# Regrouping the opening of a one-core decoder layer: groups of 2, 3, 5 and 6 row blocks instead of 2, 4, 6 and 4

## The chip, the cores and the metric

The kernel runs on 1 core of one Trainium2 chip. The metric is the device time of one execution in microseconds (us). A core has TensorE (PE; its weight loads are listed apart as PEld), VectorE (DVE), ScalarE (ACT), GpSimd (POOL) and SyncE (SP), which here only issues DMAs, and 16 DMA engines that all issuing queues share.

## The reference, cut to what matters

The layer is SwiGLU, token mixing, SwiGLU, each behind an RMS norm that is modulated by a conditioning vector c. The change lies in the first of the three:

```python
SEQ, D_MODEL, D_FF, N_MOD = 256, 2048, 5632, 9
c_act = jax.nn.silu(c)
mod = (c_act @ w_ada[l] + b_ada[l]).reshape(b, N_MOD, D_MODEL)
h = modulate(rms_norm(x, norm_ffn1[l]), mod[:, 0], mod[:, 1])
x = x + 0.5 * mod[:, 2][:, None, :] * swiglu(h, w_ffn1_gu[l], w_ffn1_down[l])
h = modulate(rms_norm(x, norm_mix[l]), mod[:, 3], mod[:, 4])
...
def swiglu(h, w_gu, w_down):
    gate, up = jnp.split(h @ w_gu, 2, axis=-1)
    return (jax.nn.silu(gate) * up) @ w_down
```

h has 256 rows and 2048 columns, that is 16 blocks of 128 columns ("row blocks" of the weight). All is float32. A matmul is made of three products of split operands: a weight tile is cast to a shorter float on ACT (the high half, `wh`), the rest is subtracted on DVE (`wl`), and TensorE adds `wh*hh`, `wh*hl` and `wl*hh`.

## The kernel before, in words

**Conditioning.** One output m (of nine) of `c_act @ w_ada` is 16 rows of w_ada's transposed layout, each 128 partitions by 2048 numbers, 1 MB. `ada_load` (L211) loads such a row, `ada_pass` (L217, its instruction is L220) multiplies a part of it by `cact` on DVE and sums it; a row takes one, two or four passes. `ada_end` (L234) adds the bias. Outputs 0 and 1 are needed block by block before h's blocks exist; outputs 2, 4 and 3 are needed later and are worked off by a pacemaker: `tick()` (L318) adds `pace["rate"]` and, for every whole one, takes a step of `conditioning` (L266), which is one pass of a quarter row and, ahead of it, the load of the row that it will want.

**The opening (L976 to L1306)** makes the first 8 of 11 column chunk pairs of h @ w_gu before all of h exists. It goes over h in groups of blocks, `bounds = (0, 2, 6, 12, 16)` (L1164). In each group the loop at L1260 visits 16 chunks of 512 columns (8 gate, 8 up; two of them are made apart in the first group). A visit loads that chunk's weights for the group's blocks (`load_blocks`, L1170, up to four blocks in a buffer), splits them in pieces of two blocks (`split`, L371: the cast is L375, the subtraction L377), and multiplies (`products`, L354, matmul L360): 6 matmuls a block. Between groups a chunk's sums are kept in SBUF: `to_parts` (L1231, copies at L1234) moves the two banks of a chunk out, and `open_banks` (L1196, copies at L1206) copies them back into PSUM before the next group adds to them. Both copies run on ACT.

**While a group is multiplied, the next group's h is made**, by the generator `group` (L1080): for each block two rows of w_ada (outputs 1 and 0), each with two passes of 1024 numbers (one of 2048 in the first group), then two blocks at a time `ada_end`, the modulation (L628) and the split of h (`parts_of_h`, L633; L636 and L637). Blocks below `TURNED = 6` are turned on TensorE (`turned_x`, L1041), later ones come turned from HBM and are scaled on POOL (`normed_columns`, L1070). The rows lie in `ring`, two places of one row each (L980). While the group before the last is multiplied (`alone`, L1249), the rows of outputs 0 and 1 use one of the two places only, since the pacemaker's rows use the other (`place`, L996, and `place_early`, L1243). In the last group the pacemaker's rows lie in weight buffers, of which there are four (`RAWS`).

**The last group** ends each pair of chunks with `swiglu_up` (L706): the kept sums are added on DVE (L720, L721), then Silu on ACT (L724), the product on DVE (L725), and the result is turned. Turned by DMA it takes three steps that `later` (L651) spreads over the following visits: ACT takes the 16-bit halves apart (L535), SP issues a DMA transpose (`back<-flat`, L540), ACT puts them together (L551). There are three `flat` and four `back` tiles. `turn_step` (L326) takes one step of all such work after every visit, and after every weight load of the later stages. The other way, `transpose_to` (L514), is four TensorE transposes (L518) and a copy out of PSUM (L519).

**Who sets the order.** SP's instructions run in the order in which the program is written (L103). The other engines' instructions are put in order by the framework's scheduler from its own times and the order of the text, and run in that order; `issue_after(i)` puts an instruction behind `i` on the same engine. Behind the opening `ffn_up` (L734) makes chunk pairs 8 to 10 with whole weights (`load`, L349) and then `down_product` (L753) follows. `Ahead` (L695) loads the first of `ffn_up`'s weights within the opening's last visit.

Accumulators are four PSUM banks (`psa`), two for each chunk.

Of the kernel before, what the change touches and what calls it, by code (L numbers as in the profile page):

```python
# [9 lines left out]
F32 = mybir.dt.float32  # L10
# [3 lines left out]
ALU = mybir.AluOpType  # L14
# [3 lines left out]
P = 128  # L18
S = 256
# [58 lines left out]
def layer_kernel(  # L78
# [615 lines left out]

    class Ahead:  # L695


        def __init__(self, raw):
            self.raw, self.made = raw, {}

        def __getitem__(self, h):
            if h not in self.made:
                self.made[h] = split(wsp, "w", self.raw[:, 2 * h : 2 * h + 2, :], CH)
            return self.made[h]

    def swiglu_up(banks_g, banks_u, tiles, ci, parts=None, by_dma=False, behind=(None, None)):  # L706

        def held_back(which):
            return nullcontext() if behind[which] is None else tc.issue_after(behind[which])

        k0 = ci * KB
        dest = tiles[k0 // KD].rearrange("p (k s) -> p k s", s=S)
        kk = k0 % KD
        work = []
        for t in range(NT):
            s = t512()
            g, u = banks_g[t], banks_u[t]
            if parts is not None:
                with held_back(1):
                    nc.vector.tensor_add(s, g, parts[0][t])  # L720
                    nc.vector.tensor_add(parts[1][t], u, parts[1][t])  # L721
                g, u = s, parts[1][t]
            with held_back(0):
# [12 lines left out]

    def ffn_up(held, w, tiles, first, bg=None, turned=(), ahead=None, head=None):
        for ci in range(first, DFF // CH):
            bg = bg or gemm(held, w, [ci * CH], ahead=head)[0]
            bu = gemm(held, w, [DFF + ci * CH], ahead=ahead)[0]  # L740
            swiglu_up(bg, bu, tiles, ci, by_dma=ci in turned)
            bg = ahead = head = None

# [296 lines left out]

    def turned_x(k0):  # L1041

        xn = [t512()[:, : 2 * P] for _ in range(NT)]
        for t in range(NT):
            nc.scalar.mul(xn[t], x_sb[:, t, k0 * P : (k0 + 2) * P], r[:, t : t + 1])
        turned = [bank()[:, :S] for _ in range(2)]
        for i in range(2):
# [21 lines left out]

    def normed_columns(k0):  # L1070

        xt = t512()
        both = xt.rearrange("p (k s) -> p k s", s=S)
        nc.sync.dma_start(both, x_t[k0 : k0 + 2].rearrange("k p s -> p k s"))
        nc.gpsimd.tensor_tensor(
            out=both, in0=both, in1=root_row[0][:, None, :].broadcast_to([P, 2, S]), op=ALU.mult
        )
        return [xt[:, i * S : (i + 1) * S] for i in range(2)]

    def group(ks, passes=2):  # L1080

        for k0 in ks[::2]:
            srcs = normed_columns(k0) if k0 >= TURNED else None
            for k in (k0, k0 + 1):
                for m in (1, 0):
                    if (m, k) not in rows_of:
                        place(m, k)
                    for q in range(passes):
                        ada_pass(k, rows_of[m, k], early[m], q, passes)
                    yield  # L1090
            for m in (1, 0):
                ada_end(m, slice(k0, k0 + 2), early[m], 0 if m else None, passes)
            h = t512()
            for i, src in enumerate(srcs or turned_x(k0)):
                modulated(h[:, i * S : (i + 1) * S], k0 + i, src, 0)
            parts_of_h(held, k0, h)

    banks, moved, unlinted, fresh = {}, set(), set(), set()
    for n, one_bank in zip(firsts, (acc_bank, side_bank)):
# [19 lines left out]
    with tc.manual_schedule(engines=ORDERED):  # L1119
# [76 lines left out]
    def open_banks(n, sums):  # L1196
        seeded = sums and n in moved
        banks[n] = [acc_bank() for _ in range(NT)]
        unlinted.discard(n)
        fresh.add(n)  # L1200
        if seeded:
            unlinted.add(n)
            fresh.discard(n)
            for b, p in zip(banks[n], part_of(n)):
                with tc.issue_after(cast[-1]):
                    nc.scalar.copy(b, p)  # L1206
# [24 lines left out]
    def to_parts(n):  # L1231
        for p, b in zip(part_of(n), banks.pop(n)):
            with tc.issue_after(cast[-1]):
                nc.scalar.copy(p, b)  # L1234
        moved.add(n)

# [11 lines left out]
    for g, ks in enumerate(groups):  # L1248
        alone.append(g == len(groups) - 2)  # L1249
        del alone[:-1]  # L1250
        final = g == len(groups) - 1
        if g == len(groups) - 2:
            set_pace(ROWS_FFN1, 192, place_early, 0)
        if final:
            pace["rate"], pace["ahead"] = 2 / 3, 1
        order = chunks if (len(groups) - g) % 2 else chunks[::-1]
# [3 lines left out]
        for i, n in enumerate(order):  # L1260
            if g == 0 and n in firsts:
                continue
            visit(n, ks, n not in stay, g == len(groups) - 2 or final and i < 12, final or (g == len(groups) - 2 and n in stay))
            if g:
# [3 lines left out]
                for m, ms in after:  # L1268
                    ready(m, ms)
                    if m not in banks and not final:  # L1270
                        open_banks(m, not (g == len(groups) - 2 and m in stay))
                if not after:
                    head = Ahead(load(gu, 0, EARLY * CH))
                    head[0]
            if final:
# [21 lines left out]
            elif n % 2:  # L1297
# [489 lines left out]
```

## Time and profile before

| | |
|---|---|
| median of 3 runs | 2366.71 us (2365.81 to 2366.98) |
| the profiled execution's own time | 2367.18 us |
| its span, first to last instruction | 2365.0 us |
| mean granted TensorE clock | 0.997 |
| DVE busy | 1672.1 us (71%) |
| ACT busy | 1373.5 us (58%) |
| HBM read | 598.47 MB, 255 GB/s over the span |
| weight loads of two and of four row blocks | 30 of 512 KB, 160 of 1024 KB |

In the tables of stretches ("windows") each row gives the stretch in us from the span's start, its length, the busy time of PE, PEld, DVE, ACT and POOL with the number of instructions, the mean granted TensorE clock, the DMA engines' busy share and the GB/s moved. In the timeline a row is: start, length, engine, line, operation, output<-input, count, and in brackets the idle time of that engine just before and what ended it. Matmuls overlap, so a matmul's length is more than its share of the stream. In lists of groups, after the bar stand the busy time in us and the mean length of one in ns.

### The profile page before, as it was taken

Reading aid. Unit: us, or ns where it says so; the run is one execution under the profiler, and the core shown is the slowest. Engines: PE = TensorE matmul, PEld = TensorE weight load, DVE = VectorE, ACT = ScalarE, POOL = GpSimd, SP = SyncE. Lnnn points to the kernel's source line nnn. Section 1 sums busy time; section 2 is a strip of 40 time slices with the busy share of each in tenths; the row PEclk is TensorE's granted clock in tenths of the full one; section 3 lists DMA queues with packets and bytes.
Section 4 is the critical chain, followed back from the end, with each engine's and each line's share of the span. In section 5 each row is a group of like instructions: output and inputs, shape, how many; then the busy total and the mean of one; then the engine's idle time right before and its main releaser. Section 6 shows DMA issues by size and latency. Waiting matters only on the chain.

```text
span 2365.0 us, 28346 instructions
## 1 busy us (share of the span) xinstructions
PE 2336.4 (99%) x10429; PEld 1917.8 (81%) x10429; DVE 1672.1 (71%) x2576; ACT 1373.5 (58%) x1900; POOL 17.4 (1%) x27
## 2 busy tenths in 40 slices
PE   8999998999999999999999999999999999999998
PEld 5888886888888888778888888888888888888887
DVE  7788886778867768975777776677655555545656
ACT  6766566555546568775556564465455455455544
POOL 0000000000000000000000000000000000000000
PEclk9999999999999999999999999999999999999999
DMA  9988979988776898877678887754767777776553
GB/s 385 375 326 352 363 240 294 373 308 318 271 259 247 265 289 230 259 226 244 267 269 307 295 288 286 289 206 185 242 238 255 251 241 256 224 235 204 193 198 125
DMA packets 196124, 631.27 MB, mean 267 GB/s; under 512 B 117329, under 2 KB 118993, under 8 KB 125457
## 3 DMA queue, kind: packets, MB, share of 16 engines
q1 hardware_dynamic: 193490, 618.46, 75.1%
q0 software_dynamic: 1600, 9.83, 1.3%
q8 instruction: 81, 1.33, 0.2%
q10 hardware_dynamic: 896, 1.19, 0.1%
q14 instruction: 57, 0.47, 0.1%
HBM read 598.47 MB, written 4.22 MB: 255 GB/s over the span
## 4 chain that ended last, share of the span: by engine, by line
PE 96%; DMA 2%; DVE 1%; ACT 1%; issue 0%; SPq 0%; DVEq 0%; ACTq 0%
PE pa L360 94%; DMA raw<-in_w_ffn_gu_dram 1%; PE ps L1471 0%; DVE slot L220 0%; DMA slot<-in_w_ada_dram 0%; PE pd L1387 0%; DMA back<-flat 0%; ACT wh L375 0%; DMA x_sb<-in_x_dram 0%; PE ps L360 0%; DVE wl L377 0%; PE ps L910 0%; PE ps L1387 0%; PE pd L1571 0%; PE pd L1556 0%
## 5 line engine op out<-in xcount | busy, mean ns | idle before, releaser
L377 DVE TENSOR_TENSOR wl<-raw,wh 128x1024 fp32r<-128x1024 f32 x792 | 963.1, 1226 | 518.8 <-ACT wh L375 452.9
L375 ACT CAST wh<-raw 128x1024 fp32r<-128x1024 f32 x792 | 829.6, 1054 | 799.9 <-PE pa L360 739.7
L360 PE MATMUL pa<-wh,hh 128*128 128x512 f32 x2184 | 599.4, 392 | 11.7 <-ACT wh L375 9.2
L360 PE MATMUL pa<-wh,hl 128*128 128x512 f32 x2184 | 594.2, 390 | 0.0
L360 PE MATMUL pa<-wl,hh 128*128 128x512 f32 x2184 | 587.7, 390 | 0.1
L360 PEld LDWEIGHTS pa<-wh,hh 128*128 128x128 f32 x2184 | 407.9, 188 | 101.7 <-ACT wh L375 13.5
L360 PEld LDWEIGHTS pa<-wh,hl 128*128 128x128 f32 x2184 | 410.4, 188 | 86.5 <-issue 0.4
L360 PEld LDWEIGHTS pa<-wl,hh 128*128 128x128 f32 x2184 | 410.0, 188 | 87.0 <-DVE wl L377 0.8
L360 PE MATMUL pa<-wh,a 128*128 128x512 f32 x1824 | 452.3, 389 | 0.0
L360 PEld LDWEIGHTS pa<-wh,a 128*128 128x128 f32 x1824 | 341.5, 188 | 70.6
L360 PE MATMUL pa<-wl,a 128*128 128x512 f32 x912 | 245.1, 389 | 0.0
L220 DVE CUSTOM_DVE_ANT_0 slot<-slot,cact 128x512 f32<-128x512 f32 (+2 forms) x292 | 221.9, 812 | 14.5 <-DMA slot<-in_w_ada_dram 14.3
L360 PEld LDWEIGHTS pa<-wl,a 128*128 128x128 f32 x912 | 171.1, 188 | 35.5
L551 ACT COPY slot<-back 128x512 uint16<-128x512 uint16 x156 | 104.0, 766 | 0.0
L535 ACT COPY flat<-t 128x512 uint16<-128x512 uint16 x144 | 81.3, 617 | 29.7 <-DMA back<-flat 21.2
L220 DVE CUSTOM_DVE_ANT_0 rows_x<-rows_x,cact 128x512 f32<-128x512 f32 x124 | 78.8, 688 | 24.7 <-DMA rows_x<-in_w_ada_dram 24.5
L410 ACT CAST a<-slot 128x512 fp32r<-128x512 f32 x114 | 70.6, 621 | 28.5 <-PE pa L360 28.3
L411 DVE TENSOR_TENSOR a<-slot,a 128x512 fp32r<-128x512 f32 x114 | 78.0, 686 | 0.1
L220 DVE CUSTOM_DVE_ANT_0 raw<-raw,cact 128x512 f32<-128x512 f32 (+1 forms) x88 | 58.2, 711 | 20.1 <-DMA raw<-in_w_ada_dram 20.1
L1234 ACT COPY slot<-pa 128x512 f32<-128x512 f32 x72 | 38.6, 589 | 22.3 <-PE pa L360 22.1
L360 PE MATMUL pa<-wh,home 128*128 128x512 f32 x160 | 39.5, 389 | 0.0
L220 DVE DVE_READ_ACCUMULATOR2_ANT sums<- 128x1 f32 x440 | 36.7, 83 | 0.0
(230 smaller groups left out, 1079.8 us busy)
## 6 DMA issues: line engine op xcount, KB each, us to landing
raw<-in_w_ffn_gu_dram SPq DMA_DIRECT2D x160, 1024.0 KB, 5.8
raw<-in_w_in_dram SPq DMA_DIRECT2D x104, 1024.0 KB, 6.2
slot<-in_w_ada_dram SPq DMA_DIRECT2D x88, 1024.0 KB, 7.3
raw<-in_w_ffn_down_dram SPq DMA_DIRECT2D x88, 1024.0 KB, 4.9
rows_x<-in_w_ada_dram SPq DMA_DIRECT2D x31, 1024.0 KB, 7.1
raw<-in_w_ada_dram SPq DMA_DIRECT2D x21, 1024.0 KB, 5.9
raw<-in_w_swa_branch_dram SPq DMA_DIRECT2D x16, 1024.0 KB, 5.7
raw<-in_w_ret_branch_dram SPq DMA_DIRECT2D x16, 1024.0 KB, 6.0
```

What stands on the lines that cost most here:

```text
L220: nc.vector.tensor_tensor_reduce(out=w[:, at], in0=w[:, at], in1=cact[:, at], scale=1.0, scalar=0.0, op0=ALU.mult, op1=ALU.add, accum_out= ...
L360: product = nc.tensor.matmul(banks[t], act[:, j, t * P : (t + 1) * P], weights[:, j, :], start=starts and i == 0 and j == 0, stop=ends and ...
L375: cast.append(nc.scalar.copy(hi, src).ins)
L377: low.append(nc.vector.tensor_sub(lo, src, hi.bitcast(F32)).ins)
L410: nc.scalar.copy(hi, v)
L411: nc.vector.tensor_sub(lo, v, hi.bitcast(F32))
L535: nc.scalar.copy(planes[:, i, :], words(src)[:, :, i])
L551: nc.scalar.copy(into[:, :, :, i], held["turned"][:, i])
L1234: nc.scalar.copy(p, b)
```

## The change

The groups become 2, 3, 5 and 6 blocks; the helpers learn to take an odd block; `TURNED` becomes 5. In the second group, four of the 16 chunks (2, 6, 10, 14) are not copied back into PSUM but start afresh, and their kept sums are added on DVE when they leave. The pacemaker runs at half a step per piece in the third group (24 passes instead of 48) and at one step per piece in the first 8 visits of the last (24 passes; before, 2/3 of a step in 12 visits of two pieces, 16 passes); the 16 passes over are left to the stages behind. In the last group the additions are no longer held behind the next visit's first subtraction (L718, L1305), pairs 6 and 7 are turned on TensorE, and `Ahead`, the early load for `ffn_up`, goes.

```diff
-        nc.scalar.copy(held.hi[:, k : k + 2, :], h)
-        nc.vector.tensor_sub(held.lo[:, k : k + 2, :], h, held.hi[:, k : k + 2, :].bitcast(F32))
+        ks = slice(k, k + h.shape[1])
+        nc.scalar.copy(held.hi[:, ks, :], h)
+        nc.vector.tensor_sub(held.lo[:, ks, :], h, held.hi[:, ks, :].bitcast(F32))
...
-    class Ahead:
...
             if parts is not None:
-                with held_back(1):
-                    nc.vector.tensor_add(s, g, parts[0][t])
-                    nc.vector.tensor_add(parts[1][t], u, parts[1][t])
+                nc.vector.tensor_add(s, g, parts[0][t])
+                nc.vector.tensor_add(parts[1][t], u, parts[1][t])
...
-    TURNED = 6
+    TURNED = 5
...
         for k0 in ks[::2]:
-            srcs = normed_columns(k0) if k0 >= TURNED else None
-            for k in (k0, k0 + 1):
+            nk = min(2, ks[-1] + 1 - k0)
+            srcs = normed_columns(k0, nk) if k0 >= TURNED else None
+            for k in range(k0, k0 + nk):
...
-    bounds = (0, 2, 6, 12, 16)
+    bounds = (0, 2, 5, 10, 16)
...
         seeded = sums and n in moved
+        if seeded and n in by_vector:
+            added.add(n)
+            seeded = False
...
         for p, b in zip(part_of(n), banks.pop(n)):
+            if n in added:
+                with tc.issue_after(low[-1]):
+                    nc.vector.tensor_add(p, p, b)
+                continue
             with tc.issue_after(cast[-1]):
                 nc.scalar.copy(p, b)
...
+        by_vector = chunks[2::4] if g == 1 else ()
         if g == len(groups) - 2:
-            set_pace(ROWS_FFN1, 192, place_early, 0)
+            set_pace(ROWS_FFN1, 2 * 192, place_early, 0)
         if final:
-            pace["rate"], pace["ahead"] = 2 / 3, 1
+            pace["rate"], pace["ahead"] = 1.0, 1
...
-            visit(n, ks, n not in stay, g == len(groups) - 2 or final and i < 12, final or (g == len(groups) - 2 and n in stay))
+            visit(n, ks, n not in stay, g == len(groups) - 2 or final and i < 8, final or (g == len(groups) - 2 and n in stay))
...
-                if not after:
-                    head = Ahead(load(gu, 0, EARLY * CH))
-                    head[0]
...
                     (part_of(n - 1), part_of(n)),
-                    True,
-                    (cast[-1], low[-1]),
+                    n // 2 < 6,
+                    cast[-1],
...
-    pace["rate"] = (192 - 64) / 117
+    pace["rate"] = (192 - 48) / 117
     pace["ahead"] = AQ
-    ffn_up(held, gu, tiles, EARLY, turned=range(EARLY, DFF // CH), head=head)
+    ffn_up(held, gu, tiles, EARLY, turned=range(EARLY, DFF // CH))
```

More of the change, by code (lines that the diff above doesn't have):

```diff
@@ L693, in later_at_once, with swiglu_up @@
                 yield
-    class Ahead:
[L698 to L709, printed above, removed]
+    def swiglu_up(banks_g, banks_u, tiles, ci, parts=None, by_dma=False, behind=None):
         k0 = ci * KB
@@ L718, in swiglu_up @@
             if parts is not None:
-                with held_back(1):
-                    nc.vector.tensor_add(s, g, parts[0][t])
-                    nc.vector.tensor_add(parts[1][t], u, parts[1][t])
+                nc.vector.tensor_add(s, g, parts[0][t])
+                nc.vector.tensor_add(parts[1][t], u, parts[1][t])
                 g, u = s, parts[1][t]
-            with held_back(0):
+            with nullcontext() if behind is None else tc.issue_after(behind):
                 nc.scalar.activation(s, g, AF.Silu)
@@ L735, in swiglu_up, with ffn_up @@
             turns.append(later(work))
-    def ffn_up(held, w, tiles, first, bg=None, turned=(), ahead=None, head=None):
+    def ffn_up(held, w, tiles, first, bg=None, turned=(), ahead=None):
         for ci in range(first, DFF // CH):
-            bg = bg or gemm(held, w, [ci * CH], ahead=head)[0]
+            bg = bg or gemm(held, w, [ci * CH])[0]
             bu = gemm(held, w, [DFF + ci * CH], ahead=ahead)[0]
             swiglu_up(bg, bu, tiles, ci, by_dma=ci in turned)
-            bg = ahead = head = None
+            bg = ahead = None
     ORDERED = {mybir.EngineType.PE, mybir.EngineType.DVE, mybir.EngineType.Activation}
@@ L1039, in square, with turned_x @@
         )
[L1041 to L1043 removed]
+    def turned_x(k0, nk=2):
+        xn = [t512()[:, : nk * P] for _ in range(NT)]
         for t in range(NT):
[L1045 to L1047 removed]
+            nc.scalar.mul(xn[t], x_sb[:, t, k0 * P : (k0 + nk) * P], r[:, t : t + 1])
+        turned = [bank()[:, :S] for _ in range(nk)]
+        for i in range(nk):
             for t in range(NT):
@@ L1091, in group @@
             for m in (1, 0):
-                ada_end(m, slice(k0, k0 + 2), early[m], 0 if m else None, passes)
-            h = t512()
-            for i, src in enumerate(srcs or turned_x(k0)):
+                ada_end(m, slice(k0, k0 + nk), early[m], 0 if m else None, passes)
+            h = t512()[:, : nk * S]
+            for i, src in enumerate(srcs or turned_x(k0, nk)):
                 modulated(h[:, i * S : (i + 1) * S], k0 + i, src, 0)
             parts_of_h(held, k0, h)
-    banks, moved, unlinted, fresh = {}, set(), set(), set()
+    banks, moved, unlinted, fresh, added = {}, set(), set(), set(), set()
     for n, one_bank in zip(firsts, (acc_bank, side_bank)):
```

11 lines of the change are left out of this document (6 added, 5 removed).

## The prediction

> **What bounds the kernel now.** I read the page first, then the busy time by stretches, then what TensorE waited for, then the timeline around the longest wait.
>
> ```profile
> PE 2336.4 (99%) x10429; PEld 1917.8 (81%) x10429; DVE 1672.1 (71%) x2576; ACT 1373.5 (58%) x1900; POOL 17.4 (1%) x27
> ```
>
> TensorE is the bound; with a span of 2365.0 us it idles 28.6 us in all, and no more can be won without taking matmuls away, which the change does not. In stretches (the opening's four groups are about 20-69, 69-156, 156-287 and 287-377):
>
> ```profile
> 20.00:69.00 49.00, 47.04 (x190) 34.36 (x189) 41.49 (x50) 35.21 (x55) 0.00 (x0) 1.00 0.98 383
> 69.00:156.00 87.00, 87.00 (x386) 72.03 (x385) 71.43 (x99) 64.69 (x97) 4.63 (x3) 1.00 0.93 368
> 156.00:287.00 131.00, 130.81 (x577) 107.81 (x576) 108.83 (x189) 77.56 (x106) 3.28 (x2) 1.00 0.88 348
> 287.00:377.00 90.00, 88.83 (x391) 72.78 (x390) 74.64 (x117) 60.89 (x81) 0.00 (x0) 1.00 0.84 263
> 377.00:408.00 31.00, 22.95 (x88) 18.41 (x89) 18.79 (x33) 19.43 (x29) 2.17 (x4) 0.83 1.01 290
> 408.00:720.00 312.00, 312.00 (x1377) 258.00 (x1377) 242.64 (x408) 172.43 (x209) 0.00 (x0) 1.00 0.83 306
> ```
>
> Between 20 and 408 TensorE idles 1.96 + 0 + 0.19 + 1.17 + 8.05 = 11.4 us; from 408 to 720 nothing. Its waits, and the largest of them in the timeline:
>
> ```profile
> PE pa L360 <- ACT wh L375: 9.2, 5, 7.3
> PE pa L360 <- DVE t L720: 1.9, 2, 1.1
> ```
> ```profile
> 393.31 1.09 PE L360 MATMUL pa<-wl,hh 128*128 128x512 f32 x4
> 401.68 2.07 PE L360 MATMUL pa<-wh,hh 128*128 128x512 f32 x4 [7.27 <-ACT wh L375]
> 403.55 1.91 PE L360 MATMUL pa<-wh,hl 128*128 128x512 f32 x4
> 405.26 1.91 PE L360 MATMUL pa<-wl,hh 128*128 128x512 f32 x4
> 406.97 1.26 PE L360 MATMUL pa<-wh,hh 128*128 128x512 f32 x4
> ```
> ```profile
> 63.49 215.32 PE pa L360 x948
> ```
> ```profile
> 396.00:400.00 4.00, 0.00 (x0) 0.00 (x0) 0.00 (x0) 1.14 (x2) 0.00 (x0) 0.64 1.12 280
> 404.00:408.00 4.00, 4.00 (x12) 3.16 (x11) 0.94 (x2) 4.00 (x6) 0.00 (x0) 0.58 1.01 305
> ```
>
> The row of 948 pieces in the chain of waits gives a matmul's share of the stream, 215.32/948 = 0.2271 us. After the four at 393.31 the next were due at 394.22; from there to 406.97 are 12.75 us, in which 12 matmuls (2.73 us) were done: the hole costs 10.0 us, 7.27 of wait and 2.7 of half clock behind it. It lies in the third and fourth weight load of `ffn_up`, right behind the opening. [...] What made this one:
>
> ```profile
> 384.69 2.66 ACT L551 COPY slot<-back 128x512 uint16<-128x512 uint16 x4
> 386.11 1.23 SPq L540 DMA_TRANSPOSE back<-flat  x1
> 386.39 0.56 POOL L306 DMA_DIRECT2D row<-gate_d  x1 [5.29 <-issue]
> 387.40 0.57 SPq L351 DMA_DIRECT2D raw<-in_w_ffn_gu_dram  x1
> 388.06 8.53 SPq L540 DMA_TRANSPOSE back<-flat  x1
> ```
> ```profile
> 387.40 13.09 DMA raw<-in_w_ffn_gu_dram
> ```
> ```profile
> raw<-in_w_ffn_gu_dram SPq DMA_DIRECT2D x160, 1024.0 KB, 5.8
> row<-gate_d POOLq DMA_DIRECT2D x1, 1024.0 KB, 10.7
> ```
>
> SP held the weight load of 387.40 behind the transpose of 386.11, and that waited for ACT to empty a `back` tile (384.69 plus two of the four copies is 386.0). It then took 13.09 us where 5.8 is the median, with POOL's 1 MB gate row and two transposes beside it. By the steps of `later` these are the transposes of pair 5.
>
> **The change, part by part.** A block in a visit is 6 matmuls, 1.363 us, so visits of 2, 3, 4, 5 and 6 blocks last 2.73, 4.09, 5.45, 6.81 and 8.18 us. The matmuls stay 16 blocks a chunk.
>
> *The hole.* The gate row leaves this place: output 2 has 48 of its 64 passes behind it, not 64, when `ffn_up` begins, and 16 more at 144/117 = 1.23 a tick are 13 ticks, 35 us on. Pairs 6 and 7 no longer queue, but pair 5's transposes stand before the same load as now. Without POOL's megabyte (1.05 MB at the 421 GB/s of the peak row below is 2.5 us) the load takes 10.6 us and TensorE waits 4.8; with the median 5.8 it lands at 393.2 and TensorE, one cast later, waits next to nothing. I take 2.5, between the two since the transposes remain: gain 7.5, bounds 10.0 and 2.5 (a wait of 4.8 with the slow clock kept).
>
> *`Ahead` gone.* Its load now stands on SP behind one more transpose (1.23 us). It was issued long before it was used, and its cast now competes on ACT with the last pair's Silu; its buffers free up three pieces ahead, so I cost it at nothing, and at one cast, about 1 us, if that cover fails.
>
> *Additions free.* The two L720 waits (1.9 us) had the additions behind a subtraction that was itself late. Gain 1.4, bounds 0 and 1.9.
>
> *First group.* Its 8 rows for the next group become 6 in the same 38 us. Idle there is 1.96 us; gain 1.5, bounds 0 and 1.96.
>
> *Turned on TensorE.* Sixteen transposes in batches of four:
>
> ```profile
> 1549.01 0.60 PE L518 MATMUL ps<-small_c,slot 128*128 128x128 f32 x4
> 1549.36 1.17 PE L360 MATMUL pa<-wh,a 128*128 128x512 f32 x4
> ```
>
> A batch holds up the stream 0.35 us: 1.4, less two transposes that block 5 no longer needs, +1.2. Behind a batch that waits for its product (L725) stand the next visit's matmuls; 0.5 us each would make it +3, the upper bound; below 1.2 nothing leads.
>
> *Second group, 87 us now 65.* Prices on DVE:
>
> ```profile
> L377 DVE TENSOR_TENSOR wl<-raw,wh 128x1024 fp32r<-128x1024 f32 x112 | 138.1, 1246 | 46.0 <-ACT wh L375 45.3 <-PE pa L360 0.4
> L220 DVE CUSTOM_DVE_ANT_0 slot<-slot,cact 128x1024 f32<-128x1024 f32 x40 | 47.3, 1220 | 0.7 <-DMA slot<-in_w_ada_dram 0.7
> L220 DVE CUSTOM_DVE_ANT_0 slot<-slot,cact 128x512 f32<-128x512 f32 x52 | 32.9, 688 | 2.6 <-DMA slot<-in_w_ada_dram 2.6
> L720 DVE TENSOR_TENSOR t<-pa,slot 128x512 f32<-128x512 f32 x12 | 7.7, 685 | 0.0
> L1206 ACT COPY pa<-slot 128x512 f32<-128x512 f32 x48 | 26.8, 592 | 0.0
> ```
>
> By busy time over count a subtraction is 1.23 us for two blocks, a row 2 x 1.18 = 2.37, a quarter pass 0.63. A visit of three blocks asks 1.85 (subtraction) + 10/14 of a row (1.69) + half an addition (0.34) = 3.9 of 4.09 us, 95%; the old visit asked 2.46 + 2.03 = 4.5 of 5.45 (82%, as the 71.43 of 87.00 show). The eight additions take 16 copies of 0.6 us, about 9 us, off ACT. DVE so near its limit costs what it cost the first group, whose rows and subtractions alone asked 8 x 2.37 + 14 x 1.23 = 36 of 38 us: 1.96 idle. I take +1.0, bounds 0 and 4.
>
> *Third group, 131 us now 109.* Here the rows for the next group use one place. Before, 8 rows in 14 visits of 8.18 us; now 12 rows in the 13 visits behind the first, 88.5 us, so 7.4 us a row. A row must land, be used (2.37 us) and only then is the next one issued; on SP, in order, the next visit's two weight loads stand behind it. What landing takes, and one quick turn of a place:
>
> ```profile
> DMA to landing us min/median/max: 4.8/8.7/11.3
> ```
> ```profile
> 193.72 0.69 DVE L220 CUSTOM_DVE_ANT_0 slot<-slot,cact 128x512 f32<-128x512 f32 x1
> 194.44 0.33 SPq L215 DMA_DIRECT2D slot<-in_w_ada_dram  x1
> 199.36 0.69 DVE L220 CUSTOM_DVE_ANT_0 slot<-slot,cact 128x512 f32<-128x512 f32 x1
> ```
> ```profile
> 240.00:250.00 10.00, 10.00 (x45) 8.11 (x44) 8.64 (x14) 6.51 (x9) 0.00 (x0) 1.00 1.01 421
> ```
>
> A turn takes 4.9 + 2.4 = 7.3 us when the row is first in the queue, 11.1 at the median. The median counts rows issued right behind two weight loads; a row that waited for its place comes behind loads that have run meanwhile, so I take 8. The bytes fit: 1.31 MB of weights, 0.97 of rows and 0.39 of the pacemaker's passes are 2.67 MB a visit, 392 GB/s where 421 is reached. With the first row about 3.5 us into the group (an estimate: it stands behind two loads that wait for half a visit's buffers), eleven turns behind it, and 7.5 us from a row's issue to the first matmul of the visit whose weights stand behind it (5.8 to land, a cast, the issues between), the last visit (due at 102 us) is late if 11 + 11 x turn > 102, that is above 8.3 us. At 8 nothing is lost, at 9 it is 8 us, at 11.1 some 31. I take +2.0, bounds 0 and 31.
>
> *Last group, 90 us now 131.* Its ACT and DVE work per us falls; its pacemaker's rows take weight buffers beside two loads a visit. +0.2, bounds 0 and 3. The 16 passes moved on are 16 x 0.63 = 10 us of DVE and 4 MB of loads, spread over 117 ticks, in stages where DVE is busy 242.64 of 312.00 and the DMA engines 0.83: nothing.
>
> The sum: -7.5 - 1.4 - 1.5 + 1.2 + 1.0 + 2.0 + 0.2 = -6.0. Against the profiled execution's 2367.18 that is 2361.2; it stood 0.5 above the median of 2366.71, so **2360.7**.
>
> **The rivals.** *One place is too few* (slower): the turn in the third group is 9 us or more and TensorE waits for weights that stand behind rows on SP. For it the 8.7 median; against it the quick turns, and that DVE waited only 0.7 us for rows. At 9.2 us a turn it costs 10 us instead of 2: 2369. It decides from 8.3 us; it turns the sign from about 9.
>
> *The hole stays*: pair 5's transposes alone hold the load. Wait 4.8 and slow clock, gain 2.5: 2365.7, no change to be seen.
>
> *Bandwidth*: the third group gets less than it asks. At the 348 GB/s that it moved on average before, a visit's 2.67 MB take 7.67 instead of 6.81 us, 11 us over 13 visits; 2372. Against it stand the 421 and the 1.01 share. [...]
>
> *The passes moved on hurt `ffn_up`*: its first stretches already have the DMA engines full (1.01 from 377 to 408). One wait of 4 us: 2364.7.
>
> That the change does not do what it says I can exclude by counting: 16 x 3 x 0.5 = 24 passes, 8 x 3 x 1 = 24.
>
> **How the numbers follow.** 0.2% is 4.7 us, about what a measurement of this kernel can tell. Forecast 0.52 (faster 0.44, same 0.08); one place too few 0.21 (slower 0.16, same 0.04, faster 0.01); hole stays 0.15 (same 0.09, faster 0.06); bandwidth 0.05 (slower 0.04, same 0.01); passes moved on 0.07 (slower 0.02, same 0.03, faster 0.02). Together faster 0.53, same 0.25, slower 0.22. The low end takes the full gains, 10.0 + 1.9 + 1.96 less 1.2 transposes: 2354.0. The high end takes the first rival to a turn of 9.5 us, 13.5 in place of 2: 2372; rarer is the rest to 31. The likeliest case alone spans 2354 to 2363.5.
>
> **What would show it.** Right: no wait above 3 us and clock 1.00 behind the opening; waits by L720 gone; 20-69 without idle; L518 16 times more at 0.35 us a batch; rows in the third group 7 to 8.3 us apart and TensorE full there. Wrong: TensorE idle by L375 late in the third group with SP held on L215 (first rival), or the same third or fourth weight load late again behind pair 5's L540.

## The result, and the profile after

The changed kernel takes 2374.07 us (median of 9 runs, 2372.00 to 2377.78) where the kernel before takes 2367.09 on the same chip (9 runs, 2365.81 to 2369.11). The ratio is 1.0032, with a 95% interval of 1.0022 to 1.0041: 7 us slower. The forecast was 2360.7 with a range up to 2372, so the sign was wrong and the time lies outside. The profiled execution took 2372.00 us, with a span of 2369.5; it is the fastest of the nine, 4.8 us over the profiled execution before, and the rest of the 7 us is not in its trace.

The page's engine line, and the stretches of the opening (the new groups are about 20-69, 69-135, 135-245 and 245-377):

```profile
PE 2339.8 (99%) x10443; PEld 1919.4 (81%) x10443; DVE 1678.4 (71%) x2610; ACT 1361.2 (57%) x1889; POOL 19.2 (1%) x28
```
```profile
20.00:69.00 49.00, 48.25 (x196) 36.20 (x195) 37.31 (x46) 34.68 (x55) 0.00 (x0) 1.00 0.94 361
69.00:135.00 66.00, 64.17 (x280) 51.88 (x279) 58.32 (x94) 48.88 (x81) 4.02 (x3) 1.00 0.92 358
135.00:245.00 110.00, 103.30 (x440) 83.30 (x439) 89.79 (x156) 66.11 (x100) 5.69 (x3) 0.97 0.86 338
245.00:377.00 132.00, 129.26 (x568) 106.07 (x567) 98.03 (x149) 72.13 (x91) 0.00 (x0) 1.00 0.81 264
377.00:408.00 31.00, 31.00 (x147) 25.75 (x146) 26.59 (x44) 26.48 (x38) 0.00 (x0) 1.00 0.95 295
408.00:720.00 312.00, 312.00 (x1379) 258.31 (x1378) 249.57 (x435) 166.16 (x199) 2.16 (x4) 1.00 0.87 319
```

Busy against length: the hole from 377 to 408 is gone. In its place TensorE idles 1.83 us in the second group, 6.70 in the third, where the mean clock is 0.97, and 2.74 in the last. What it waits for has changed too. Line numbers are now those of the changed kernel: the copies of L1206 stand at L1196 there, the weight loads of `load_blocks` at L1160. No wait by the additions (L720 before) is left, and the largest is by ACT's copies of kept sums into PSUM:

```profile
PE pa L360 <- ACT pa L1196: 6.9, 5, 4.0
...
PE pa L360 <- DVE wl L377: 3.3, 2, 1.7
...
PE pa L360 <- ACT wh L375: 1.7, 3, 0.9
```

Idle time leaves out slow matmuls. How far the stream has come is better read from the number of matmuls of L360 since 27 us (the first x of a row). Before:

```profile
27.00:69.00 42.00, 39.21 (x164) 30.11 (x164) 1.00 0.98 376
27.00:135.00 108.00, 105.21 (x455) 84.76 (x455) 1.00 0.93 365
27.00:245.00 218.00, 215.21 (x941) 175.82 (x941) 1.00 0.91 357
27.00:377.00 350.00, 345.85 (x1512) 282.64 (x1511) 1.00 0.89 334
27.00:440.00 413.00, 400.80 (x1740) 327.28 (x1740) 0.99 0.91 334
```

After:

```profile
27.00:69.00 42.00, 40.47 (x172) 31.79 (x172) 1.00 0.92 352
27.00:135.00 108.00, 104.64 (x450) 83.67 (x450) 1.00 0.92 355
27.00:245.00 218.00, 207.94 (x888) 166.98 (x888) 0.98 0.89 347
27.00:377.00 350.00, 337.20 (x1454) 273.05 (x1454) 0.99 0.86 316
27.00:440.00 413.00, 399.18 (x1723) 323.29 (x1723) 0.99 0.88 322
```

The changed kernel is 8 matmuls ahead at 69 us, 5 behind at 135, 53 at 245, 58 at 377, and 17 at 440. At the prediction's 0.2271 us each: the first group gains 1.8 us, the second loses 2.9, the third 10.9, the last 1.1, and the hole behind the opening, less the 1.4 us of TensorE transposes that fall into the same stretch, gives back 41 matmuls or 9.3 us. The 17 that are left are 3.9 us; the spans differ by 4.5.

**The third group, read closely.** The first passes of the first and of the last of the twelve rows that come through the one place (each row takes two passes), and between them the longest wait in the timeline:

```profile
147.56 1.22 DVE L220 CUSTOM_DVE_ANT_0 slot<-slot,cact 128x1024 f32<-128x1024 f32 x1
...
226.51 1.22 PE L360 MATMUL pa<-wh,hh 128*128 128x512 f32 x2 [3.98 <-ACT pa L1196]
...
244.51 1.22 DVE L220 CUSTOM_DVE_ANT_0 slot<-slot,cact 128x1024 f32<-128x1024 f32 x1
```

So eleven turns took 244.51 - 147.56 = 96.95 us, 8.81 each. The chain of waits into that matmul, and SP's queue beside it:

```profile
206.13 4.82 DMA slot<-in_w_ada_dram
...
214.27 10.55 DMA raw<-in_w_ffn_gu_dram
...
224.92 0.43 ACT wh L375
...
225.87 0.59 ACT pa L1196
...
226.51 8.62 PE pa L360 x27
```
```profile
213.38 0.80 SPq L215 DMA_DIRECT2D slot<-in_w_ada_dram  x2
214.27 1.12 SPq L1160 DMA_DIRECT2D raw<-in_w_ffn_gu_dram  x2
```

A row issued at 206.13 lands after 4.82 us, is used by DVE until 213.34, and only then does SP issue the next row, at 213.38 (together with one of the pacemaker's), and behind it the weights of 214.27. Those land 10.55 us later, where 5.8 was the median before; two rows and two weight loads leave together here. The copies of kept sums that TensorE is said to wait for stand on ACT behind the cast of these weights; they aren't the cause. The eleven turns are far from equal: three took 7.24 to 7.25 us, four took 9.17 to 14.17. In the longest, the row issued at 191.96 followed two weight loads of 188.61 and took 10.01 us to land. And the wait costs more than its 3.98 us, as the granted clock (the column behind POOL's) shows:

```profile
222.00:226.00 4.00, 0.53 (x2) 0.09 (x1) 2.79 (x10) 1.08 (x2) 0.00 (x0) 0.80 1.01 414
226.00:230.00 4.00, 3.49 (x8) 2.84 (x9) 3.29 (x4) 3.44 (x6) 0.00 (x0) 0.50 0.69 286
230.00:234.00 4.00, 4.00 (x16) 3.23 (x15) 3.19 (x5) 2.48 (x4) 0.00 (x0) 0.85 0.70 224
```

### The profile page after: what moved, and what is told of

It reads as the page before. It is cut to its first block, busy times and chain, and to the rows that moved or that the text cites. A ratio compares the mean times of both kernels' runs of the same rounds, so it can differ in the third digit from the quotient of the medians.

```text
span 2369.5 us, 28452 instructions
## 1 busy us (share of the span) xinstructions
PE 2339.8 (99%) x10443; PEld 1919.4 (81%) x10443; DVE 1678.4 (71%) x2610; ACT 1361.2 (57%) x1889; POOL 19.2 (1%) x28
## 4 chain that ended last, share of the span: by engine, by line
PE 93%; DMA 3%; DVE 2%; ACT 1%; issue 1%; SPq 0%; DVEq 0%; ACTq 0%
PE pa L360 91%; DMA raw<-in_w_ffn_gu_dram 2%; DMA raw<-in_w_ada_dram 1%; PE ps L1464 0%; ACT wh L375 0%; DVE slot L220 0%; DVE wl L377 0%; PE pd L1380 0%; DVE raw L220 0%; DMA x_sb<-in_x_dram 0%; DMA back<-flat 0%; PE ps L360 0%; PE pa L1101 0%; ACT pa L1196 0%; ACT slot L1228 0%
## 5 line engine op out<-in xcount | busy, mean ns | idle before, releaser
L377 DVE TENSOR_TENSOR wl<-raw,wh 128x1024 fp32r<-128x1024 f32 (+1 forms) x808 | 962.2, 1201 | 519.8 <-ACT wh L375 458.2
L375 ACT CAST wh<-raw 128x1024 fp32r<-128x1024 f32 (+1 forms) x808 | 832.6, 1037 | 824.2 <-PE pa L360 753.0
L360 PE MATMUL pa<-wh,hh 128*128 128x512 f32 x2184 | 601.4, 392 | 9.3 <-ACT pa L1196 6.9
L360 PE MATMUL pa<-wh,hl 128*128 128x512 f32 x2184 | 595.6, 390 | 0.0
L360 PE MATMUL pa<-wl,hh 128*128 128x512 f32 x2184 | 589.1, 390 | 3.3 <-DVE wl L377 3.3
L360 PEld LDWEIGHTS pa<-wh,hh 128*128 128x128 f32 x2184 | 407.6, 188 | 99.6 <-ACT pa L1196 9.2
L360 PEld LDWEIGHTS pa<-wl,hh 128*128 128x128 f32 x2184 | 409.7, 188 | 91.6 <-DVE wl L377 5.7
L360 PEld LDWEIGHTS pa<-wh,hl 128*128 128x128 f32 x2184 | 410.4, 188 | 86.4 <-issue 0.4
L360 PE MATMUL pa<-wh,a 128*128 128x512 f32 x1824 | 452.1, 389 | 0.0
L360 PEld LDWEIGHTS pa<-wh,a 128*128 128x128 f32 x1824 | 341.7, 188 | 70.5
L360 PE MATMUL pa<-wl,a 128*128 128x512 f32 x912 | 245.1, 389 | 0.0
L220 DVE CUSTOM_DVE_ANT_0 slot<-slot,cact 128x512 f32<-128x512 f32 (+2 forms) x282 | 214.6, 810 | 14.4 <-DMA slot<-in_w_ada_dram 14.1
L360 PEld LDWEIGHTS pa<-wl,a 128*128 128x128 f32 x912 | 171.1, 188 | 35.4
L551 ACT COPY slot<-back 128x512 uint16<-128x512 uint16 x148 | 98.7, 766 | 0.0
L220 DVE CUSTOM_DVE_ANT_0 raw<-raw,cact 128x512 f32<-128x512 f32 (+1 forms) x100 | 65.6, 708 | 23.9 <-DMA raw<-in_w_ada_dram 23.9
L360 PE MATMUL pa<-wh,home 128*128 128x512 f32 x160 | 39.5, 389 | 0.0
```

What stands on the lines that cost most here:

```text
L220: nc.vector.tensor_tensor_reduce(out=w[:, at], in0=w[:, at], in1=cact[:, at], scale=1.0, scalar=0.0, op0=ALU.mult, op1=ALU.add, accum_out= ...
L360: product = nc.tensor.matmul(banks[t], act[:, j, t * P : (t + 1) * P], weights[:, j, :], start=starts and i == 0 and j == 0, stop=ends and ...
L375: cast.append(nc.scalar.copy(hi, src).ins)
L377: low.append(nc.vector.tensor_sub(lo, src, hi.bitcast(F32)).ins)
L551: nc.scalar.copy(into[:, :, :, i], held["turned"][:, i])
```

## The experiments

Every ratio is against the kernel before on the same chip, whose median lay between 2366.7 and 2367.1 us in all these comparisons.

### What is short in the third group

My theory after the result was that SP's order is at fault: weights stand behind a row that waits for its place. The first run moves that waiting to GpSimd's queue.

```diff
-        ada_load(m, k, rows_of[m, k], 2 if k < 2 else 1)
+        ada_load(m, k, rows_of[m, k], 2 if k < 2 else 1, nc.gpsimd if alone[0] else None)
```

> The changed kernel, but the twelve rows of outputs 0 and 1 in the third group are issued on POOL's queue; still one place, same passes. Theory (one place, and weights held behind rows on SP): the weight loads go early, TensorE's idle time in the third group (6.7 us of 110) falls below 2 us, total some 7 to 9 us less than the changed kernel, about 2366. Rival (the third group simply asks more of the DMA engines and DVE than they give): idle stays at 5 to 7 us, total 2373 to 2375.

Measured: 2373.19 us, ratio 1.0033 (1.0021 to 1.0045); nothing is won. GpSimd issued eleven rows between 135 and 250 us, the first and the last at

```profile
146.41 0.53 POOL L215 DMA_DIRECT2D slot<-in_w_ada_dram  x1 [12.75 <-DVE sums L220]
...
248.83 0.53 POOL L215 DMA_DIRECT2D slot<-in_w_ada_dram  x1 [10.13 <-DVE sums L220]
```

which is ten turns of 10.2 us, and now DVE itself waits for a row, with the subtraction for TensorE behind that row's passes:

```profile
189.20 1.22 DVE L220 CUSTOM_DVE_ANT_0 slot<-slot,cact 128x1024 f32<-128x1024 f32 x1 [5.29 <-DMA slot<-in_w_ada_dram]
...
191.50 2.35 DVE L377 TENSOR_TENSOR wl<-raw,wh 128x1024 fp32r<-128x1024 f32 x2
```

TensorE waited 5.99 us for that subtraction. So SP's order only decides where a late row is felt: here the subtraction of 191.50 came behind the pass of 189.20 on DVE. A place turned in 8.81 us from SP's queue and in 10.2 from GpSimd's, and TensorE was held up with both.

The next two take the pacemaker's 24 passes out of the group (they are made up behind the opening), the second with both places for the rows besides.

```diff
+            pace["rate"] = 0.0
...
-    pace["rate"] = (192 - 48) / 117
+    pace["rate"] = (192 - 24) / 117
```

> The changed kernel without the pacemaker's 24 passes in the third group (they go to the stages behind, 168/117 a tick); one place. Theory (one place): a turn of the place shortens only by the traffic that is gone, from 8.8 to about 8.3 us, so a part of the loss stays: total 2368 to 2371. Rival (load): with 6 MB and 15 us of DVE less the third group fills, total 2364 to 2366.

```diff
-        alone.append(g == len(groups) - 2)
+        alone.append(False)
...
+            pace["rate"] = 0.0
...
-    pace["rate"] = (192 - 48) / 117
+    pace["rate"] = (192 - 24) / 117
```

> As the run with no passes and one place, but the rows take both places in turn. Theory (one place): TensorE full in the third group, 3 to 6 us faster than with one place, total 2363 to 2366. Rival (load): no faster than with one place, within 1 us.

Measured: 2370.39 us, ratio 1.0011 (1.0002 to 1.0021), and 2366.18 us, ratio 0.9999 (0.9989 to 1.0008). The third group of the first and of the second:

```profile
135.00:245.00 110.00, 108.08 (x473) 88.14 (x472) 80.81 (x117) 70.79 (x107) 6.03 (x3) 1.00 0.82 306
```
```profile
135.00:245.00 110.00, 110.00 (x487) 91.05 (x486) 84.72 (x121) 73.67 (x108) 4.44 (x3) 1.00 0.86 321
```

Without the pacemaker the one place turns in 8.13 us, TensorE idles 1.92 us, and 14 matmuls (3.2 us) are missing against the run with two places, in which the group is full, with as many matmuls (487) as before had in the same stretch. The second place is worth 4.2 us of time. The pacemaker's absence is worth 3.7, though its passes then cost 2.95 us of idle time between 408 and 720. With the pacemaker's passes and rows the turn is 8.81 us, without them 8.13; what part of their price acts other than through the turn, by their bytes or their time on DVE, these runs can't tell apart.

One more run loads each row of this group in two halves, so that a half can be used and refilled earlier.

```diff
-        ada_load(m, k, rows_of[m, k], 2 if k < 2 else 1)
+        ada_load(m, k, rows_of[m, k], 2 if k < 2 or alone[0] else 1)
```

> The changed kernel, but each row of outputs 0 and 1 in the third group is loaded as two halves of 1024 columns, so that a half is issued when its own pass has ended and not when both have: same bytes, same passes, same place. Theory (the turn of the one place decides): the turn shortens by up to one pass, 1.2 us, from 8.8 to 7.6 to 8.2 us; the third group loses 3 us or less in place of 9 to 11; total 2366 to 2369. Rival (bytes and DVE work): unchanged, 2373 to 2375.

Measured: 2370.84 us, ratio 1.0015 (1.0006 to 1.0024). I had expected a turn of 7.6 to 8.2 us and 2366 to 2369, and missed both: from the first pass of the first row (147.74) to that of the last (243.45) a turn took 8.70 us. By the times the run is 3.2 us better than the change, but its interval overlaps the change's, and its profile shows no gain: 6.73 us idle between 135 and 245, a span of 2368.9. It settles nothing.

### The groups' sizes, the last group and the second

Groups of 2, 4, 5 and 5 keep the second group as it was, give the third 10 rows to fetch in place of 12, and all other edits stay.

```diff
-    TURNED = 5
+    TURNED = 6
...
-    bounds = (0, 2, 5, 10, 16)
+    bounds = (0, 2, 6, 11, 16)
...
-        by_vector = chunks[2::4] if g == 1 else ()
+        by_vector = ()
```

> The changed kernel with groups of 2, 4, 5 and 5: the third group has to make ten rows, not twelve, in the same 13 visits of 6.8 us, 8.9 us a row; no additions in place of copies. Theory (one place with a turn of about 8.8 us is too few for 7.4 us a row): the third group fills, TensorE idle there under 2 us; total 2357 to 2361. Rival (visits of five blocks load DVE and the DMA engines too much as such): 4 us or more idle there, 2363 to 2368.

The next is the same kernel without the pacemaker in its last group.

```diff
-            pace["rate"], pace["ahead"] = 1.0, 1
+            pace["rate"], pace["ahead"] = 0.0, 1
...
-    pace["rate"] = (192 - 48) / 117
+    pace["rate"] = (192 - 24) / 117
```

> The changed kernel with groups of 2, 4, 5, 5, no additions in place of copies, and besides no pacemaker in the last group (its 24 passes go to the stages behind the opening). Theory (the pacemaker's rows in the weight buffers are what the last group loses by, 3.6 us with them): its idle time falls under 1 us and the kernel comes to 2362 to 2364 us, against 2365.8 with them; up to 1 us of it may be given back behind the opening, where the passes go. Rival (five blocks in two loads a visit from four buffers are too many by themselves): the idle time stays above 2.5 us and the time at 2365 to 2367.

Measured: 2365.76 us, ratio 0.9997 (0.9987 to 1.0006), and 2363.36 us, ratio 0.9984 (0.9974 to 0.9993). Third and last group of the first, then the last group and the stages behind the opening of the second:

```profile
156.00:265.00 109.00, 107.47 (x475) 88.69 (x474) 90.26 (x155) 70.65 (x107) 5.12 (x3) 1.00 0.86 332
265.00:378.00 113.00, 109.44 (x477) 88.01 (x476) 89.95 (x147) 67.02 (x96) 0.00 (x0) 1.00 0.82 271
```
```profile
265.00:378.00 113.00, 113.00 (x505) 93.64 (x504) 78.48 (x103) 73.36 (x103) 0.00 (x0) 1.00 0.69 223
...
408.00:720.00 312.00, 309.05 (x1360) 254.46 (x1359) 262.42 (x476) 165.79 (x199) 2.17 (x4) 1.00 0.88 335
```

With ten rows the third group loses 1.5 us, as the theory says. I had expected 2357 to 2361 in all, and missed that: 3.6 us are lost in the last group, and the second run shows to what, since it is full without the pacemaker's rows in its weight buffers. But 24 more passes behind the opening cost 2.95 us there. So the passes can be moved, and the stage that takes them pays most of what the other saves.

The last of this group takes the additions on DVE back in the second group of the changed kernel.

```diff
-        by_vector = chunks[2::4] if g == 1 else ()
+        by_vector = ()
```

> The changed kernel with the second group's four chunks copied back into PSUM by ScalarE again, no additions on VectorE in their place. Theory (VectorE at 95% is what the second group of three blocks loses by): with 5.5 us of additions gone from it that group loses 1 us in place of some 2.7, and the time is 2371 to 2373 us; the third group stays as it was. Rival (ScalarE's nine more us in 66 make it late instead): the second group loses as much or more than now, waits on ScalarE's copies (L1206) show, and the time is 2374 to 2377 us.

Measured: 2375.20 us, ratio 1.0034 (1.0021 to 1.0047), the same time as with the additions. The second group idles 2.01 us in place of 1.83. So the additions are neutral. That DVE's load as a whole costs the group nothing isn't shown: the run took only 3.2 us off DVE (58.32 to 55.13 us busy in 66) and put 7.0 on ACT (48.88 to 55.86). The rival's range of time was met, but its sign, waits for ACT's copies, doesn't appear in the group. What TensorE waits for longest there is a subtraction of L377 in both, 1.64 us up to 129.66 in the changed kernel and 1.23 up to 129.04 in this run. Ahead of it on DVE stands this row, first in the changed kernel, then in this run:

```profile
124.87 0.69 DVE L638 TENSOR_TENSOR hl<-t,hh 128x512 fp32r<-128x512 f32 x1 [2.20 <-ACT hh L637]
```
```profile
124.25 0.69 DVE L638 TENSOR_TENSOR hl<-t,hh 128x512 fp32r<-128x512 f32 x1 [2.52 <-ACT hh L637]
```

DVE stands over 2 us for ACT's cast of the next group's h, with two row passes and the next subtraction queued behind it in order. On ACT that cast comes behind the modulation (L628) and copies of sums out of PSUM, which in the changed kernel had waited 1.67 us for TensorE (until 118.80). No run moves that cast, so this reason is argued from the traces alone.

### The hole behind the opening

Four runs on the kernel before and one on the changed one. First all edits at the end of the last group, with before's groups: the early load gone, pairs 6 and 7 turned on TensorE, additions free.

```diff
-                if not after:
-                    head = Ahead(load(gu, 0, EARLY * CH))
-                    head[0]
...
-                    True,
-                    (cast[-1], low[-1]),
+                    n // 2 < 6,
+                    (cast[-1], None),
```

> The kernel before (groups of 2, 4, 6 and 4, its passes) with only the edits in the last group: additions free, pairs 6 and 7 turned on TensorE, no early load. By the prediction's reading (the hole hangs on pair 5's transposes and POOL's megabyte, which both stay) a wait of 4 us or more stays behind the opening and the total is 2364 to 2368. Rival (the queue of pairs 6 and 7, or the additions held back, made the hole): no wait there, 8 to 10 us less, 2357 to 2360.

Then two of these edits by themselves, the transposes and the additions:

```diff
-                    True,
+                    n // 2 < 6,
                     (cast[-1], low[-1]),
```

> The kernel before with one edit: pairs 6 and 7 turned on TensorE (four DMA transposes fewer in the first weight loads of ffn_up); additions still held back, early load kept. The last-group edits together took 9.3 us. Theory (the DMA transposes of the late pairs, queued with the weight loads on SP and in the DMA engines, made the hole): most of it, 6 to 9 us: 2358 to 2361. Rival (the additions held behind a late subtraction made it): 0 to 3 us: 2364 to 2367.

```diff
                     True,
-                    (cast[-1], low[-1]),
+                    (cast[-1], None),
```

> The kernel before with one edit: the additions in the last group no longer held behind the next visit's first subtraction; all pairs turned by DMA, early load kept. Theory (the DMA transposes made the hole): the two L720 waits of 1.9 us go, the hole stays: 2364 to 2367. Rival (the order on DVE made it): 6 to 9 us less: 2358 to 2361.

Measured: 2357.43 us, ratio 0.9960 (0.9945 to 0.9975); 2359.62 us, ratio 0.9967 (0.9954 to 0.9979); 2363.80 us, ratio 0.9987 (0.9978 to 0.9996). The first is faster than both kernels, by 9.3 us than the one before and by 16.6 than the changed one; by the prediction's reading a wait should have stayed (2364 to 2368), so that expectation was missed. With the two pairs on TensorE the stretch from 378 to 408 is full (30.00 of 30.00 in both runs); with the additions alone a hole of 5.2 us stays there, and the gain lies ahead of it (1522 matmuls at 377 in place of 1512, 2.3 us).

I read that as the transposes alone making the hole. But in the runs with two pairs on TensorE GpSimd's 1 MB gate row had also moved, from 386.39 to 402.74 and, with all three edits, to 403.83, though no edit touches it. So the next run moves the gate row and leaves the transposes.

```diff
-            pace["rate"], pace["ahead"] = 2 / 3, 1
+            pace["rate"], pace["ahead"] = 0.0, 1
...
-    pace["rate"] = (192 - 64) / 117
+    pace["rate"] = (192 - 48) / 117
```

> The kernel before with one thing moved: the pacemaker rests in the last group, and its 16 passes are made up behind the opening. So the end of output 2, and with it GpSimd's 1 MB gate row, comes some 35 us later than the hole, while all eight pairs are still turned by DMA. Theory of the runs so far (the hole is made by the transposes of the last two pairs on SyncE's queue): the weight load behind the opening is late again, TensorE idles at least 4 us between 378 and 408, and the time is 2364 to 2368 us. Rival (the gate row's megabyte, as the prediction had it): the load takes under 8 us, TensorE idles less than 2 us there, and the time is 2357 to 2360 us.

Measured: 2360.21 us, ratio 0.9974 (0.9964 to 0.9984), 0.2 us above the rival's range and 3.8 below the theory's. All eight pairs are turned by DMA, the gate row leaves at 407.74, and

```profile
378.00:408.00 30.00, 29.23 (x129) 23.85 (x128) 25.42 (x48) 24.38 (x38) 0.80 (x2) 1.00 1.04 355
```

TensorE idles 0.77 us. Neither the transposes nor the gate row make the hole by themselves. The last run has the changed kernel's groups with before's end of the last group, so that the two meet again at another time.

```diff
+                if not after:
+                    head = Ahead(load(gu, 0, EARLY * CH))
+                    head[0]
...
-                    n // 2 < 6,
-                    cast[-1],
+                    True,
+                    (cast[-1], low[-1]),
...
-    ffn_up(held, gu, tiles, EARLY, turned=range(EARLY, DFF // CH))
+    ffn_up(held, gu, tiles, EARLY, turned=range(EARLY, DFF // CH), head=head)
```

> The changed kernel with the groups 2, 3, 5, 6, the additions of the second group and its rates of the pacemaker, but with the edits at the end of the last group taken back: additions and Silu held as before, all eight pairs turned by DMA, the early load for the stage behind kept. Theory (the two halves of the change add up): the groups alone lose some 58 matmuls of 0.227 us, 13 us, up to the end of the last group, and the hole behind the opening comes back with 8 to 10 us; 2376 to 2382 us, so slower than before by 0.4 to 0.65%. Rival (visits of six blocks leave the DMA transposes time enough, and the hole goes by the regrouping alone): 2371 to 2374 us and TensorE full within 1 us between 378 and 408.

Measured: 2380.28 us, ratio 1.0055 (1.0040 to 1.0070), as the theory that the halves add up expected. TensorE is full from 378 to 408, as the rival expected, but the time isn't the rival's. The groups alone cost 13.2 us and the last edits alone gain 9.3; their sum, 3.9 slower, agrees with the change's 7.0 within the intervals, each some 2 to 4 us to either side. The hole hasn't gone; it has moved with the gate row:

```profile
421.26 1.24 SPq L540 DMA_TRANSPOSE back<-flat  x1
422.55 0.57 SPq L351 DMA_DIRECT2D raw<-in_w_ffn_gu_dram  x1
422.78 0.56 POOL L306 DMA_DIRECT2D row<-gate_d  x1 [4.87 <-DMA gate_d<-t]
423.21 4.88 SPq L540 DMA_TRANSPOSE back<-flat  x1
...
436.73 2.07 PE L360 MATMUL pa<-wh,hh 128*128 128x512 f32 x4 [5.14 <-ACT wh L375]
```

By the chain of waits the load of 422.55 took 12.98 us, as that of 387.40 took 13.09 in the kernel before; with the additions alone the load of 384.48, 0.6 us behind the gate row, took 11.78. What happens while they meet, in this run and in the kernel before, and with a gate row that meets no transposes (the run with two pairs on TensorE); the last two columns are the DMA engines' share and the GB/s:

```profile
423.00:429.00 6.00, 6.00 (x28) 4.95 (x28) 5.56 (x13) 2.00 (x2) 1.41 (x3) 1.00 1.16 227
```
```profile
387.00:393.00 6.00, 6.00 (x28) 4.99 (x27) 4.81 (x11) 2.72 (x4) 1.02 (x2) 1.00 1.11 131
```
```profile
403.00:409.00 6.00, 6.00 (x28) 4.99 (x27) 5.90 (x12) 5.27 (x7) 1.36 (x3) 1.00 1.00 415
```

The engines are taken all the time and move 131 or 227 GB/s, where the gate row beside plain loads leaves 415. One meeting did no such harm: in the run that moves it, the gate row came at 407.74, 0.5 us behind a weight load with a transpose right behind it; the engines moved 393 GB/s from 408 to 414, that load took 8.64 us and TensorE waited less than 1 us. So a meeting isn't enough by itself. What else it takes, and where in the engines the time goes, stays open.

## Why the prediction was wrong, point by point

*The third group: the step that failed.* "A row that waited for its place comes behind loads that have run meanwhile, so I take 8." The turn measured 8.81 us. What failed is the reason given for 8: in the four long turns the row took 6.6 to 10.0 us to land, where it took 4.8 in the three quick ones, so it did not come behind loads that had run meanwhile. The formula beside it, 11 + 11 x turn against 102, holds within 2 us for idle time: at 8.81 it gives 5.9 us and the stretch from 135 to 245 idles 6.70. The other runs with one place on SP's queue bear it out.

| run | turn, us | 11 + 11 x turn - 102 | idle 135 to 245, us |
|---|---|---|---|
| no pacemaker in the group | 8.13 | below 0 | 1.92 |
| changed kernel | 8.81 | 5.9 | 6.70 |
| groups only | 8.97 | 7.7 | 7.31 |
| no additions in the second group | 9.00 | 8.0 | 7.94 |

So the mechanism was right, named as the first rival, and the size of the turn was wrong by a tenth; the threshold of 8.3 us is softer than the prediction had it, since 8.13 already idles 1.92. Each 0.1 us of a turn above the threshold is 1.1 us of lateness, so by the formula that tenth accounts for 5.9 us where 2.0 were forecast and 10.9 measured. I had the pacemaker's passes in the sum of the bytes and not in the turn; without them it measured 8.13, and the group did 33 matmuls (7.5 us) more. The second part of the miss is the price of lateness, which the prediction put at its own length. The half clock behind the longest wait adds 2.3 us to the 6.70 of idle time (last section), and the other 1.9 us of the 10.9 show in no idle time, and where they lie stays open.

*The second group.* Forecast +1.0, bounds 0 and 4; 13 matmuls or 2.9 us were lost. The size lies in the bounds. The reason given for it (DVE at 95%) isn't borne out: DVE was busy 58.32 of 66 us, 88%, and with the additions taken off it the group loses the same. That the loss lay within the bounds is then luck.

*The hole.* Forecast -7.5, measured 41 matmuls with the transposes' 1.4 us paid, that is -10.7: all 10.0 us, the bound, and most of a wait by L720 of 1.10 us that stood at 377.78 in the kernel before and so in the same stretch. The two causes named, POOL's megabyte and transposes on SP's queue, were the right ones, but in this kernel the later gate row wasn't the cure: with the same groups and all pairs turned by DMA it met transposes again at 422.78, and what the change adds to that run is the two pairs on TensorE, free additions and no early load. The 2.5 us held back for pair 5's transposes were too careful: without the gate row beside them TensorE idles at most 0.77 us from 378 to 408. The rival "the hole stays" is refuted.

*The first group, the bank waits, the transposes, the last group, `Ahead`.* The first group gained 1.8 (forecast 1.5). The additions left free gained 2.3 us of matmuls where they were the only edit of the last group (forecast 1.4, bound 1.9), more than the waits in the profile showed. A batch of four transposes holds the stream as long as forecast: in the changed kernel one starts at 380.75 and the matmul behind it at 381.10, 0.35 us. The last group lost 1.1 (forecast 0.2, bounds 0 and 3), to the pacemaker's rows in weight buffers as named, which the runs show for groups of 2, 4, 5 and 5 only. Nothing was lost where `Ahead` stood.

*The other rivals.* Bandwidth over the group, as priced, doesn't explain the loss: the third group moved 338 GB/s on average, less than the 348 before, and 414 while TensorE waited for the weights; with two places, and without the 6 MB of the passes, it is full. The passes moved on cost nothing as the change moves them (16 of them; 312.00 of 312.00 busy from 408 to 720), and 2.95 us when 24 more follow.

*The sum.* By matmuls: -1.8 + 2.9 + 10.9 + 1.1 - 9.3 = +3.8 us, against -6.0 forecast. Of the difference of 9.8, 8.9 are the third group's.

## What to carry to other kernels

A buffer with a single place has a turn, landing plus use plus whatever stands ahead on the engine that uses it, and its whole chain is that turn times the rows (here 96.95 us for eleven turns of 8.81): take the turn from rows that carry the same company as the new stage, and when the forecast lies within a tenth of the threshold, price the other side of it in the sum and not only as a rival. Passes with no due time still need a stage with room; here 24 of them taken out of one stage were paid for in a later one, with 2.95 us of idle time. A transfer that was late because two queues met was cured here by moving either (TensorE idled 0.77 us or nothing from 378 to 408), unless they met again later (a wait of 5.14 us up to 436.73), so before blaming one of them look whether the cure also moved the other.

## What the runs showed of the hardware

Half clock followed waits of 3.98, 2.66 and 2.55 us in these runs, and a wait's length alone didn't decide. In the changed kernel 3.98 us of waiting were followed by 0.50 of full speed from 226 to 230 us: 12 matmuls from 226.51 to 231.54 took 5.03 us where 2.73 were due, 2.3 us on top of the wait. The clock was at 0.50 from 224.39, within that wait, to 231.21, and in the kernel before from 397.11, within the wait of 7.27 us, to 407.34. Shorter waits were followed by half clock too. With the rows on GpSimd's queue a wait of 2.66 us was followed by the first row below, and without additions in the second group one of 2.55 us (at 180.15) by the other:

```profile
232.00:236.00 4.00, 3.51 (x9) 2.83 (x10) 3.81 (x5) 2.05 (x3) 0.00 (x0) 0.61 1.03 381
```
```profile
180.00:184.00 4.00, 3.85 (x10) 3.03 (x11) 2.27 (x3) 3.08 (x6) 2.01 (x1) 0.57 1.00 421
```

In the changed kernel the waits of 1.64 (up to 129.66) and 1.66 us (up to 311.36) left the clock at 1.00. With the rows in halves TensorE idled only 1.93 us in all from 265 to 378, and yet the clock was at 0.50 in the first row below. Without additions in the second group a wait of 2.25 us (312.09 to 314.34), in the other two rows, left the clock at 1.00:

```profile
311.82:315.22 3.40, 3.40 (x10) 2.63 (x9) 3.40 (x5) 0.40 (x1) 0.00 (x0) 0.50 0.86 293
```
```profile
310.25:313.65 3.40, 1.84 (x9) 1.18 (x7) 3.04 (x9) 0.27 (x1) 0.00 (x0) 1.00 0.48 195
313.66:317.07 3.41, 2.73 (x12) 2.28 (x13) 3.41 (x5) 1.76 (x2) 0.00 (x0) 1.00 0.68 226
```

What decides beside the length isn't shown. The prediction priced the third group's lateness at its own length, 8 us at a turn of 9; a wait of 3.98 us there cost 2.3 us more than that.
